# Three TensorE rows of eight instead of four, one uncut last store, and a 1 KB extra store, in a rotary-embedding kernel that streams through memory

## The chip, the core and the metric

The kernel runs on one core of a Trainium2 chip. The metric is device time in microseconds (us). Every quoted time is a median over several executions, each of state "fast", that is, undisturbed. One execution of every kernel was also recorded with the hardware profiler; its "span" runs from the first to the last instruction, and is 1.7 to 2.3 us shorter than the time of the same execution. Engines are named as in the profile: PE is TensorE, PEld its weight loads, DVE is VectorE, ACT is ScalarE, POOL is GpSimd, and SPq is the sequencer of SyncE, which issues the transfers ("DMA").

## The reference

The input `x` is 16 x 512 x 1024 float32, seen as 16 heads of 64. Each head is rotated by a table of cosines and sines of its position:

```python
x1, x2 = x[..., :32], x[..., 32:]          # per head, after the reshape to 16 heads of 64
rotated = np.concatenate([x1 * cos - x2 * sin, x1 * sin + x2 * cos], axis=-1)
```

32 MiB come in and 32 MiB go out, and there is little arithmetic for each byte.

## The kernel before

The work is cut into 8 tiles of 128 partitions x 8192 floats (4 MB). A tile has 8 "rows" of 1024 floats per partition. Each row needs two products and an add: `x * cos`, the half-swapped `x * sin` with signs, and their sum. The rows are spread over the engines in two ways:

```python
PE_ROWS = (0, 2, 4, 6)          # rows whose sum TensorE makes
DVE_B = ((0,), (0, 4))          # rows (even tiles, odd tiles) whose sine product VectorE makes; else GpSimd
LAST_OUT = (4, 8)               # the last tile is stored in two pieces, rows 0-3 and rows 4-7
...
for t in range(NT):
    xt = tiles[t]
    for k in range(KK):
        r = xt[:, k * dim : (k + 1) * dim]
        own = k in DVE_B[t % 2]
        if not own:
            ... nc.gpsimd.tensor_tensor(out=halves(b), ...)                # sine product on GpSimd
        if k in PE_ROWS:
            ps = pe.tile([P, dim], FP32, name="ps")                        # two buffers in PSUM
            nc.vector.tensor_tensor(out=pairs(ps), in0=pairs(r), in1=cos_b(k), op=ALU.mult)
            if own:
                nc.vector.tensor_tensor(out=halves(r), ...)                # sine product on VectorE
            ... nc.tensor.matmul(out=ps[...], lhsT=ident, rhs=rhs, start=False, ...)   # adds it into ps
            nc.scalar.copy(out=r, in_=ps)                                  # ScalarE brings the row back
            while pending: add()
        else:
            while pending: add()
            ps = pd.tile([P, dim], FP32, name="pd")                        # one buffer in PSUM
            nc.vector.tensor_tensor(out=pairs(ps), in0=pairs(r), in1=cos_b(k), op=ALU.mult)
            pending.append((r, ps, b))                                     # add() later: r = ps + b on VectorE
    while pending: add()
    ... store(t)                                                           # the last tile by LAST_OUT
```

All loads and stores are issued by SyncE on one queue. Five tile buffers exist, so tiles 5 to 7 are loaded when the stores of tiles 0 to 2 have landed.

## Time and profile before

| | before |
|---|---|
| time, median of 5 | 163.11 us (163.08 to 163.17) |
| span of the profiled run | 161.6 us |
| data moved on the load/store queue | 67.24 MB |
| VectorE ends its last operation | 142.97 us |
| last store issued (its second half) | 143.03 us |
| last data lands | 160.5 us |

These lines are from the page of the kernel before: busy time by engine, three rows of the 40 slices of the span (a digit is the busy share in tenths; PEclk is the granted TensorE clock in tenths), and the queue that carries loads and stores (packets, MB, share of the 16 DMA engines' span).

```profile
PE 81.8 (51%) x136; PEld 30.3 (19%) x136; DVE 128.9 (80%) x115; ACT 33.7 (21%) x33; POOL 121.0 (75%) x58
...
DVE  1059897999999989999999999999999999930000
...
PEclk9999996559975998799969965999689879995555
DMA  5999999999999999999999999999999999999992
...
q1 hardware_dynamic: 2752, 67.24, 97.5%
```

VectorE, the busiest compute engine, is busy for 80% of the span. The DMA row shows 9 from the second slice to the last but one, while VectorE stops four slices (16 us) earlier. The kernel is bound by the transfers. In the packet records a 32 KB packet takes 1.213 us, and a 4 MB transfer puts 8 of them on each of the 16 engines: 9.7 us per transfer, and sixteen such transfers make 155 us.

The second reading is how much room compute has. The timeline of the kernel before, from 139 us (columns: start, duration, engine and line, operation, operands, count, and in brackets the idle time before it and what ended it):

```profile
139.39 1.96 PE L168 MATMUL ps<-b,ident 128*128 128x512 f32 x4 [1.57 <-DVE ps L163]
...
141.43 1.01 ACT L171 COPY xt<-ps 128x1024 f32<-128x1024 f32 x1 [2.56 <-PE ps L168]
141.74 1.22 DVE L150 TENSOR_TENSOR xt<-pd,b 128x1024 f32<-128x1024 f32 x1
143.03 0.33 SPq L79 DMA_DIRECT2D out_dram<-xt  x1
```

Compute ends at 142.97 us. The store of tile 6 lands at 149.1 to 150.8 us, so the queue gets to the last tile only around 149, and to its second half, the transfer issued at 143.03, about 5 us later. The last tile waits in the queue; the queue doesn't wait for it.

### The profile page before, as it was taken

Reading aid. Unit: us, or ns where it says so; the run is one execution under the profiler, and the core shown is the slowest. Engines: PE = TensorE matmul, PEld = TensorE weight load, DVE = VectorE, ACT = ScalarE, POOL = GpSimd, SP = SyncE. Lnnn points to the kernel's source line nnn. Section 1 sums busy time; section 2 is a strip of 40 time slices with the busy share of each in tenths; the row PEclk is TensorE's granted clock in tenths of the full one; section 3 lists DMA queues with packets and bytes.
Section 4 is the critical chain, followed back from the end, with each engine's and each line's share of the span. In section 5 each row is a group of like instructions: output and inputs, shape, how many; then the busy total and the mean of one; then the engine's idle time right before and its main releaser. Section 6 shows DMA issues by size and latency. Waiting matters only on the chain.

```text
span 161.6 us, 692 instructions
## 1 busy us (share of the span) xinstructions
PE 81.8 (51%) x136; PEld 30.3 (19%) x136; DVE 128.9 (80%) x115; ACT 33.7 (21%) x33; POOL 121.0 (75%) x58
## 2 busy tenths in 40 slices
PE   4136946496429742955097419660984194600000
PEld 1112301241114211311032114210321131100000
DVE  1059897999999989999999999999999999930000
ACT  0003242023302430223113302222223122220000
POOL 1049999999999999999994199999999997000000
PEclk9999996559975998799969965999689879995555
DMA  5999999999999999999999999999999999999992
GB/s 189 395 441 435 454 454 389 446 462 389 438 470 389 389 446 464 389 454 446 397 454 446 397 448 446 406 454 438 406 450 438 406 448 438 414 454 389 438 426 118
DMA packets 2756, 67.28 MB, mean 416 GB/s; under 512 B 320, under 2 KB 448, under 8 KB 448
## 3 DMA queue, kind: packets, MB, share of 16 engines
q1 hardware_dynamic: 2752, 67.24, 97.5%
q8 instruction: 1, 0.02, 0.0%
q14 instruction: 3, 0.02, 0.0%
HBM read 33.69 MB, written 33.55 MB: 416 GB/s over the span
## 4 chain that ended last, share of the span: by engine, by line
DVE 37%; PE 18%; issue 17%; POOL 6%; ACT 4%; DMA 4%; SPq 0%; DVEq 0%; ACTq 0%; POOLq 0%
PE ps L168 17%; DVE xt L150 12%; DVE pd L178 12%; DVE ps L163 7%; POOL b L160 6%; DVE xt L165 5%; ACT xt L171 4%; DMA b<-in_sin_dram 4%; PE tab L110 1%; PE tab L111 1%; DVE tab L118 0%; DVE sns L113 0%; SPq L75 0%; DVE sns L114 0%; DVEq L150 0%
## 5 line engine op out<-in xcount | busy, mean ns | idle before, releaser
L160 POOL TENSOR_TENSOR b<-xt,sns 128x1024 f32<-128x1024 f32 x52 | 120.3, 2350 | 14.5 <-DVE sns L114 9.2
L168 PE MATMUL ps<-xt,ident 128*128 128x512 f32 x48 | 35.8, 888 | 39.2 <-issue 24.5
L171 ACT COPY xt<-ps 128x1024 f32<-128x1024 f32 x32 | 32.4, 1012 | 95.2 <-PE ps L168 90.8
L168 PE MATMUL ps<-b,ident 128*128 128x512 f32 x80 | 43.5, 674 | 14.7 <-DVE ps L163 12.1
L150 DVE TENSOR_TENSOR xt<-pd,b 128x1024 f32<-128x1024 f32 x32 | 39.0, 1218 | 2.2 <-POOL b L160 1.1
L163 DVE TENSOR_TENSOR ps<-xt,tab 128x1024 f32<-128x1024 f32 x32 | 39.1, 1223 | 1.5 <-ACT xt L171 1.3
L178 DVE TENSOR_TENSOR pd<-xt,tab 128x1024 f32<-128x1024 f32 x32 | 39.3, 1227 | 0.8
L168 PEld LDWEIGHTS ps<-b,ident 128*128 128x128 f32 x80 | 17.1, 227 | 44.1 <-issue 30.6
L168 PEld LDWEIGHTS ps<-xt,ident 128*128 128x128 f32 x48 | 11.6, 267 | 58.8 <-issue 46.1
L165 DVE TENSOR_TENSOR xt<-xt,tab 128x1024 f32<-128x1024 f32 x12 | 14.6, 1220 | 0.4
L113 DVE TENSOR_SCALAR sns<-tab 128x256 f32<-128x256 f32 x1 | 0.4, 425 | 8.0 <-PE tab L111 8.0
L171 ACT ACT_TABLE_LOAD x1 | 1.3, 1283 | 13.5 <-DVE xt L165 13.5
L110 PE MATMUL tab<-b,spread 64*128 64x256 f32 x2 | 1.2, 697 | 4.5 <-DMA b<-in_sin_dram 4.5
L101 PE MATMUL ps<-zero 128*128 128x512 bf16 x4 | 1.9, 625 | 1.2 <-DVE zero L97 1.2
L110 PEld LDWEIGHTS tab<-b,spread 64*128 64x128 f32 x2 | 0.5, 308 | 5.4 <-issue 5.4
L111 PE MATMUL tab<-b,spread 64*128 64x256 f32 x2 | 1.1, 631 | 0.0
L97 DVE MEMSET zero<- 128x256 uint32 x1 | 0.3, 272 | 0.9 <-PEq L208 0.9
L101 PEld LDWEIGHTS <-zero 128*128 128x128 bf16 x4 | 0.4, 129 | 1.7 <-DVE zero L97 1.2
L111 PEld LDWEIGHTS tab<-b,spread 64*128 64x128 f32 x2 | 0.7, 333 | 0.2
L118 DVE COPY tab<-sns 128x64 f32<-128x64 f32 x2 | 0.5, 228 | 0.1
L109 DVE COPY spread<-ident 64x64 f32<-64x64 f32 x2 | 0.3, 182 | 0.2 <-POOL ident masks.py:199 0.2
masks.py:197 POOL MEMSET ident<- 128x128 f32 x1 | 0.2, 204 | 0.3 <-POOLq L208 0.3
(6 smaller groups left out, 1.1 us busy)
## 6 DMA issues: line engine op xcount, KB each, us to landing
xt<-in_x_dram SPq DMA_DIRECT2D x7, 4096.0 KB, 29.5
out_dram<-xt SPq DMA_DIRECT2D x7, 4096.0 KB, 30.3
out_dram<-xt SPq DMA_DIRECT2D x2, 2048.0 KB, 18.1
xt<-in_x_dram SPq DMA_DIRECT2D x1, 2560.0 KB, 11.3
xt<-in_x_dram SPq DMA_DIRECT2D x1, 1536.0 KB, 6.2
b<-in_sin_dram SPq DMA_DIRECT2D x1, 64.0 KB, 6.3
b<-in_cos_dram SPq DMA_DIRECT2D x1, 64.0 KB, 6.1
```

The source lines that it names most:

```text
L101: nc.tensor.matmul(out=ps[:, c : c + BANK], lhsT=zero[:, :P], rhs=zero, start=True, stop=True)
L110: nc.tensor.matmul(out=sin_t, lhsT=spread, rhs=sin_sb, start=True, stop=True)
L111: nc.tensor.matmul(out=cos_t, lhsT=spread, rhs=cos_sb, start=True, stop=True)
L113: nc.vector.tensor_scalar_mul(out=sns[:, :, 0, :], in0=sin_k, scalar1=-1.0)
L118: nc.vector.tensor_copy(out=sns_t[:, i * hd : (i + 1) * hd], in_=sns[:, k])
L150: nc.vector.tensor_tensor(out=r, in0=ps, in1=b, op=ALU.add)
L160: nc.gpsimd.tensor_tensor(out=halves(b), in0=swapped(r, nh), in1=over_heads(sk), op=ALU.mult)
L163: nc.vector.tensor_tensor(out=pairs(ps), in0=pairs(r), in1=cos_b(k), op=ALU.mult)
L165: nc.vector.tensor_tensor(out=halves(r), in0=halves(r), in1=swapped_signed(k), op=ALU.mult)
L168: nc.tensor.matmul(out=ps[:, c : c + BANK], lhsT=ident, rhs=rhs, start=False, stop=True, skip_group_check=True)
L171: nc.scalar.copy(out=r, in_=ps)
L178: nc.vector.tensor_tensor(out=pairs(ps), in0=pairs(r), in1=cos_b(k), op=ALU.mult)
```

## The change

Its intent: fewer rows go through TensorE and ScalarE, so that the adds of one more row per tile run on VectorE; the store of the last tile isn't cut; and a 1 KB store of zeros goes out on ScalarE's own queue at the start. The tables' loads are written more plainly, with the same two transfers.

```diff
-PE_ROWS = (0, 2, 4, 6)
+PE_ROWS = (0, 3, 6)
-DVE_B = ((0,), (0, 4))
+DVE_B = ((0,), (0, 3))
-LAST_OUT = (4, 8)
+LAST_OUT = (8,)
-SIN_PARTS = (64,)
-COS_PARTS = (64,)
...
+    zero = fixed.tile([P, BANK], BF16)
+    nc.vector.memset(zero, 0.0)
+    scratch = nc.dram_tensor("scratch", (16, 32), BF16, kind="Internal").ap()
+    nc.scalar.dma_start(out=scratch, in_=zero[:16, :32])
     load(0, 0, FIRST[0])
...
-    zero = fixed.tile([P, BANK], BF16)
-    nc.vector.memset(zero, 0.0)
```

VectorE gets 8 more adds (123 instructions for 115). TensorE has 96 matmul records for rows instead of 128, ScalarE 24 copies instead of 32. GpSimd keeps its 52 products.

More of the change, by code (lines that the diff above doesn't have):

```diff
@@ L83 @@
     cos_sb = bp.tile([P, dim], FP32, name="b")[:PB, : KK * half]
-    for sb, v, parts in ((sin_sb, sin_v, SIN_PARTS), (cos_sb, cos_v, COS_PARTS)):
-        lo = 0
-        for hi in parts:
-            nc.sync.dma_start(out=sb[lo:hi, :], in_=v[lo:hi, :])
-            lo = hi
+    nc.sync.dma_start(out=sin_sb, in_=sin_v)
+    nc.sync.dma_start(out=cos_sb, in_=cos_v)
     for lo, hi in zip(FIRST, FIRST[1:]):
```

## The prediction

> **What bounds the kernel now.** The DMA queue. The page's queue lines give 67.24 MB on one queue, filling 97.5% of the 16 engines' span; the DMA row of the slices is 9 nearly throughout. In the packet records 32 KB takes 1.213 us, so a 4 MB transfer (8 packets per engine) takes 9.7 us, and sixteen make 155 of the 161.6 us. VectorE (80%) and GpSimd (75%) only have to stay ahead. At the end the timeline of SyncE shows the last tile's halves issued at 136.9 and 143.0 us, VectorE ending at 142.97. The queue only gets to the last tile near 148 us (the store before it lands at 149.1 to 150.8), and to its second half near 153. Compute has about 10 us of slack.
>
> **What the change does.**
> - PE rows 2, 4, 6 become 3, 6: one row per tile moves its final add from TensorE and ScalarE to VectorE, 8 more adds. GpSimd keeps 52 products. In the timeline VectorE's operations follow each other at 1.13 us, 1.25 us when one needs the previous one's buffer, 1.33 us when an add directly follows its own product. The new order then makes 17.1 us for an even tile and 18.3 for an odd one, against 15.4 and 16.8 in the last two of before. Tile 0 loses nothing, because GpSimd paces it (products 2.31 us apart). Tiles start at 28.0, 46.4, 63.4, 81.8, 98.8, 117.2, 134.2; VectorE ends near 152.7, 9.7 us later.
> - The earlier stores and reloads still reach the queue in time (store 6 issued near 135, needed near 138).
> - The last tile's row 6 on TensorE starts near 149.1 us after some 4 us idle. Before, bursts after 4.1 us of idle nearly all ran at 0.85 us per matmul, not 0.43. This agrees with the Trainium skill, "TensorE: Matmul & The Clock Gate", Part 1 (half rate after about 3.4 us idle). Then matmuls take 3.7 us and the copy 1.0, ending near 153.9; if warm, VectorE is last at 152.7.
> - One 4 MB last store: nothing leaves until then. Alone it would cost nothing (143 is before 148); with the later compute the queue is empty for 5 to 6 us.
> - The 1 KB store: 16 rows of 64 B on ScalarE's queue, idle until 13.5 us. By the skill's "DMA: Bandwidth & Descriptors", "Issuing engines are not separate DMA queues", it interleaves on the same 16 engines; a 1 KB packet of the tables took 0.046 us here. Under 0.2 us.
>
> **Time.** Store issued 152.7 to 154.0, rather the later; 1.0 us to the first packet (first load: issue 0.73, packet 1.74), 0.5 start-up (first packets took 1.0 us, not 0.46), 9.7 data, 0.4 to the semaphore, 1.1 to the span's end, 1.5 from span to measured time (163.1 against 161.6). That is issue plus 14.2: 166.9 to 168.2. I predict 167.8 us, +2.9%, 8 in 10 between 166.3 and 168.8. Faster by over 2%: 0.01; within 2%: 0.14; slower by over 2%: 0.85.
>
> **What would show it.** VectorE's last add ends near 152.7, ScalarE's last copy after it, the last store is issued near 154; the DMA row dips for 5 to 6 us near 149 to 155, then is full to the end, and 9 elsewhere; 96 row matmuls instead of 128; ScalarE's queue under 0.1%.
>
> **What would make it wrong.** Smaller gaps on VectorE, or GpSimd running differently beside it (1 us of compute is 1 us of time); a warm last burst; the small store disturbing the start.

## The result, and the profile after

| | before | after |
|---|---|---|
| time, median of 5 | 163.11 us (163.08 to 163.17) | 168.19 us (168.02 to 168.40) |
| span of the profiled run | 161.6 us | 166.3 us |
| VectorE ends | 142.97 us | 152.97 us |
| last store issued | 143.03 us | 154.12 us |
| last data lands | 160.5 us | 165.2 us |

The ratio is 1.031, with a 95% interval of 1.030 to 1.033. Ratios here are the mean time of one kernel's fast runs over the mean of the other's fast runs in the same rounds, so they are not quite the ratios of the medians quoted beside them.

The same lines of the page, for the changed kernel (q10 is ScalarE's queue with the 1 KB store):

```profile
PE 83.4 (50%) x104; PEld 26.1 (16%) x104; DVE 139.6 (84%) x123; ACT 25.6 (15%) x25; POOL 121.4 (73%) x58
...
DVE  1069999999999999999999999999999999997000
...
PEclk9999999556785678655559855858555955556755
DMA  6999989898999999999999999999999999960885
...
q1 hardware_dynamic: 2608, 67.24, 94.6%
...
q10 hardware_dynamic: 32, 0.00, 0.0%
```

Three things are to be seen. TensorE was granted its full clock less often (mean 0.69, before 0.83). VectorE works on for two slices and a half longer. And the DMA row has a 6 and a 0 where it had 9s: the queue ran empty near the end, then carried the last store alone. The windows view puts numbers to it. First the kernel before, then the changed one (columns: window, its length, busy us and count of PE, PEld, DVE, ACT, POOL, granted clock, DMA share, GB/s):

```profile
149.00:156.00 7.00, 0.00 (x0) 0.00 (x0) 0.00 (x0) 0.00 (x0) 0.00 (x0) 0.50 0.99 426
156.00:162.00 6.00, 0.00 (x0) 0.00 (x0) 0.00 (x0) 0.00 (x0) 0.00 (x0) 0.50 0.45 191
```

```profile
149.00:156.00 7.00, 3.61 (x4) 1.17 (x4) 3.83 (x4) 1.01 (x1) 0.00 (x0) 0.73 0.17 75
156.00:167.00 11.00, 0.00 (x0) 0.00 (x0) 0.00 (x0) 0.00 (x0) 0.00 (x0) 0.51 0.78 334
```

Between 149 and 156 us the DMA engines were 99% busy before and are 17% busy now, with compute still running in that window. In the packet records the last packets of tile 6's store end at 149.0 us on average over the 16 engines (start 147.8 plus 1.213), the latest at 149.5, and the first packets of tile 7's store begin at 155.0: a hole of 6.0 us on average. The span grew by 4.7 us only, because the slowest engine ends it. Before, the engines had drifted apart, and the last packet ended at 160.1 us, 1.2 us after the mean of the 16 engines' ends (158.9). After the hole all engines start together, and the last packet ends at 164.9, 0.1 us after the mean (164.8). So 1.1 of the 6.0 us are made up by this evening out, 0.2 by tile 6's store having ended earlier (149.0 on average, before 149.2), and the other 4.7 are the growth. The windows view of the changed kernel, which counts a packet where it starts, shows none from 148.4 to 154.9 us:

```profile
148.40:154.90 6.50, 3.61 (x4) 1.17 (x4) 4.43 (x4) 1.01 (x1) 0.00 (x0) 0.67 0.00 0
```

What ended last in the last tile is read from the timeline of the changed kernel:

```profile
149.40 3.61 PE L164 MATMUL ps<-b,ident 128*128 128x512 f32 x4 [2.37 <-DVE ps L159]
...
151.74 1.22 DVE L146 TENSOR_TENSOR xt<-pd,b 128x1024 f32<-128x1024 f32 x1
153.09 1.01 ACT L167 COPY xt<-ps 128x1024 f32<-128x1024 f32 x1 [5.01 <-PE ps L164]
154.12 0.33 SPq L76 DMA_DIRECT2D out_dram<-xt  x1
```

VectorE ends at 152.97 us, but the store waits for ScalarE's copy of row 6, which ends at 154.10, because the four matmuls before it took 3.61 us. The same four took 1.96 us before. This is the half-rate state of the clock, which the Trainium skill describes in "TensorE: Matmul & The Clock Gate", Part 1. The granted clock in the trace is 0.50 until 152.74 us.

### The profile page after: what moved, and what is told of

The parts are those of the page before. It is cut to its first block, busy times and chain, and to the rows that moved or that the text cites. A ratio compares the mean times of both kernels' runs of the same rounds, so it can differ in the third digit from the quotient of the medians.

```text
span 166.3 us, 610 instructions
## 1 busy us (share of the span) xinstructions
PE 83.4 (50%) x104; PEld 26.1 (16%) x104; DVE 139.6 (84%) x123; ACT 25.6 (15%) x25; POOL 121.4 (73%) x58
## 4 chain that ended last, share of the span: by engine, by line
DVE 71%; issue 13%; DMA 4%; PE 3%; ACT 1%; DVEq 0%; SPq 0%; ACTq 0%
DVE pd L174 29%; DVE xt L146 23%; DVE ps L159 10%; DVE xt L161 9%; DMA b<-in_sin_dram 4%; PE ps L164 2%; PE tab L106 1%; ACT xt L167 1%; PE tab L107 1%; DVEq L146 0%; DVE tab L114 0%; DVE sns L109 0%; SPq L72 0%; DVE sns L110 0%; DVEq L161 0%
## 5 line engine op out<-in xcount | busy, mean ns | idle before, releaser
L164 PE MATMUL ps<-xt,ident 128*128 128x512 f32 x48 | 41.6, 1018 | 36.2 <-issue 21.1
L164 PE MATMUL ps<-b,ident 128*128 128x512 f32 x48 | 37.9, 934 | 27.5 <-DVE ps L159 17.2
L146 DVE TENSOR_TENSOR xt<-pd,b 128x1024 f32<-128x1024 f32 x40 | 48.9, 1221 | 2.5
L174 DVE TENSOR_TENSOR pd<-xt,tab 128x1024 f32<-128x1024 f32 x40 | 49.1, 1228 | 1.1
L167 ACT COPY xt<-ps 128x1024 f32<-128x1024 f32 x24 | 24.3, 1012 | 114.8 <-PE ps L164 100.3
L159 DVE TENSOR_TENSOR ps<-xt,tab 128x1024 f32<-128x1024 f32 x24 | 29.3, 1222 | 0.0
L164 PEld LDWEIGHTS ps<-xt,ident 128*128 128x128 f32 x48 | 12.9, 296 | 63.6 <-issue 58.8
L164 PEld LDWEIGHTS ps<-b,ident 128*128 128x128 f32 x48 | 11.7, 268 | 54.4 <-POOL b L156 28.0
```

Source lines behind the costliest of these rows:

```text
L146: nc.vector.tensor_tensor(out=r, in0=ps, in1=b, op=ALU.add)
L164: nc.tensor.matmul(out=ps[:, c : c + BANK], lhsT=ident, rhs=rhs, start=False, stop=True, skip_group_check=True)
```

## The experiments

Theory: the loss is what two parts of the change make together. VectorE's additional adds make the last tile ready some 10 us later, and the uncut store lets nothing of it leave before all of it is ready; only then does the queue run empty. Rivals: (A) the later compute costs its time anyway; (B) the small store, or the lower granted clock with fewer rows on TensorE, costs it; (C) a 4 MB last store costs time by itself. All runs gave the right result, and the kernel before ran beside each (medians 163.25 to 163.32 us).

### One part at a time

**e1_split_last**: the changed kernel, with the store cut again.

```diff
-LAST_OUT = (8,)
+LAST_OUT = (4, 8)
```

> The changed kernel with the last store cut in two again (rows 0-3, rows 4-7). Theory (the loss is the product of later compute and an uncut last store): the first half is issued near 148.1 us, the second near 154.1 as in the changed kernel, but only 4.9 us of data remain behind it; span near 161.8, time 163.4 to 164.0, so -2.6% against the changed kernel. Rival A (the later compute alone costs the time): 167 to 168.2. Rival B (the small store or the lower granted clock costs it): 167.5 to 168.2.

Measured: 163.42 us, ratio to before 1.001 (0.999 to 1.003). VectorE still ends at 152.99 us, and the halves are issued at 147.81 and 153.27. The two windows for this kernel:

```profile
149.00:156.00 7.00, 2.73 (x4) 0.71 (x4) 3.85 (x4) 1.01 (x1) 0.00 (x0) 0.60 0.95 405
156.00:162.00 6.00, 0.00 (x0) 0.00 (x0) 0.00 (x0) 0.00 (x0) 0.00 (x0) 0.50 0.48 205
```

With as late a compute, the DMA share in 149 to 156 us is back at 0.95, because rows 0 to 3 keep the queue busy while rows 4 to 7 are made. Rivals A and B fall: the later compute, the lower clock and the small store are all still there.

**e2_before_one_store**: the kernel before, with the store in one piece.

```diff
-LAST_OUT = (4, 8)
+LAST_OUT = (8,)
```

> The kernel before with nothing changed but the last store in one piece. Theory: it is issued at 143.0 us, the queue gets to it only near 148, so nothing is lost: 163.0 to 163.3. Rival C (one 4 MB store at the end costs time by itself, by its longer tail): 165 to 168.

Measured: 163.17 us, ratio 0.999 (0.998 to 1.001). The store was issued at 143.72 us, and tile 6's store landed at 148.9 to 150.5. Rival C falls. So neither part costs anything alone, and together they cost 5 us.

**e3_before_small_store** and **e4_after_no_small_store**: the 1 KB store put into the kernel before, and taken out of the changed kernel.

```diff
     # e3, into the kernel before (its zeros are made here instead of later):
+    scratch = nc.dram_tensor("scratch", (16, 32), BF16, kind="Internal").ap()
+    nc.scalar.dma_start(out=scratch, in_=zero[:16, :32])
     # e4, out of the changed kernel:
-    scratch = nc.dram_tensor("scratch", (16, 32), BF16, kind="Internal").ap()
-    nc.scalar.dma_start(out=scratch, in_=zero[:16, :32])
```

> The kernel before with nothing changed but the 1 KB store (and its zeros made earlier). Theory: the tables land up to 0.2 us later, the queue stays full: span within 0.2 us of 161.6, time 163.1 to 163.3. Rival D (the second queue costs something outside the span: in the changed kernel time less span was about 2.0 us against 1.8): 163.4 to 163.8 with the span unchanged. Rival B (the small store is the cause): 166 or more.

> The changed kernel without the 1 KB store. Theory: the start is 0.2 us earlier, so the last store is issued near 153.9: time 167.8 to 168.1. Rival D: 167.4 to 167.8. Rival B: 163 to 165.

Measured: e3 163.22 us, ratio 0.999 (0.998 to 1.001); e4 168.35 us, ratio 1.030 (1.028 to 1.032), against 1.031 with the store. e4 is 0.25 us over the range that I named: its last store was issued at 154.24 us, not near 153.9, so leaving the small store out gained nothing at the end. The small store costs nothing that can be seen, inside the span or outside it (rival D of these expectations falls too).

### Which engine is last

**e5_last_row5**: the changed kernel, with row 5 in place of row 6 on TensorE in the last tile alone.

```diff
-            if k in PE_ROWS:
+            if k in ((0, 3, 5) if t == NT - 1 else PE_ROWS):
```

> The changed kernel with rows 0, 3, 5 instead of 0, 3, 6 on TensorE in the last tile alone: as many operations on every engine. Theory (the last store waits for ScalarE's copy after a half-rate burst, 154.1 us, while VectorE is done at 152.97): now VectorE's last add, near 153.0, is last: the last store is issued 1.0 to 1.2 us earlier, time 167.0 to 167.3. Rival (VectorE's end alone sets it and the copy is a bystander): 168.0 to 168.4.

Measured: 167.23 us, ratio 1.024 (1.023 to 1.026). From the timeline of this kernel:

```profile
149.51 1.01 ACT L167 COPY xt<-ps 128x1024 f32<-128x1024 f32 x1 [1.50 <-PE ps L164]
...
151.67 1.23 DVE L146 TENSOR_TENSOR xt<-pd,b 128x1024 f32<-128x1024 f32 x1
152.96 0.33 SPq L76 DMA_DIRECT2D out_dram<-xt  x1
```

Now ScalarE's copy is done at 150.52 us and VectorE is last. The store leaves 1.16 us earlier and the time falls by 0.96 us. So about 1 us of the 5 is the slow last burst on TensorE with the copy behind it, and the rest is VectorE's.

### How much delay is free

**e6_first4** and **e7_first6**: three rows in the first 4 or 6 tiles only, four rows (with the division of work of before) in the rest; the store uncut.

```diff
-PE_ROWS = (0, 3, 6)
+def pe_rows(t):
+    return (0, 3, 6) if t < THREE_UNTIL else (0, 2, 4, 6)      # THREE_UNTIL = 4 in e6, 6 in e7
...
-DVE_B = ((0,), (0, 3))
+def dve_b(t):
+    return (0,) if t % 2 == 0 else (0, 3) if t < THREE_UNTIL else (0, 4)
...
```

> The changed kernel with three rows on TensorE in tiles 0 to 3 and the four of before in tiles 4 to 7; last store in one piece. Theory of the slack: compute ends near 147.3 us, and the queue is busy with the store before until 148.6 to 149.5, so half of the delay costs nothing: 163.0 to 163.5. Rival (each extra add costs its share, linear in the number of tiles): half of 5.1 us, 165.6.

> The same with three rows in tiles 0 to 5 and four in tiles 6 and 7. Theory: compute ends near 150.0 us, 0.8 us to the first packet, about 1.5 us of empty queue: span near 162.2, time 163.7 to 164.3. Rival (linear): 6/8 of 5.1 us, 166.9.

Measured: e6 163.28 us, ratio 1.000 (0.999 to 1.001); e7 164.51 us, ratio 1.007 (1.006 to 1.009), 0.2 us over the range named. Half of the tiles cost nothing, two more cost 1.2 us, and the last two 3.7. The cost isn't a sum over tiles; it begins at a threshold.

**e9_idle_vector_op**: the kernel before with its four rows, the store uncut, and one idle product per tile on VectorE. It tests whether VectorE's time alone does it, with TensorE's work as it was.

```diff
+    junk = fixed.tile([P, dim], FP32)
+    nc.vector.memset(junk, 0.0)
...
+            if k == 3:
+                nc.vector.tensor_tensor(out=pairs(junk), in0=pairs(junk), in1=cos_b(k), op=ALU.mult)
```

> The kernel before, four rows on TensorE, last store in one piece, no 1 KB store; one idle VectorE product per tile on a tile of zeros that nobody reads. Theory (VectorE's own time moves the last store, whatever TensorE does): compute ends 7 to 8 us later than with one store alone (143.7), near 150.7 to 151.7; last store issued then; 12.2 us to the span's end and 1.8 more: time 164.7 to 165.8. Rival (taking rows off TensorE, with the lower granted clock, is what costs time): 163.1 to 163.4, as with one store alone.

Measured: 163.06 us, ratio 0.998 (0.997 to 1.000). My expectation was wrong: VectorE ended at 148.58 us, not 150.7 to 151.7. The starts of its operations in the trace show why. I had put the idle product between an add and a product that had to wait for that add's buffer. Before, the product followed the add after 1.25 us; now all steps there are 1.13, so an idle product adds 1.01 us where it stands, and in several tiles it also filled a wait for ScalarE. The store was issued at 148.64 us, in time. The run can't tell the theory from the rival.

**e11_idle_vector_more**: the same with four more idle products, so that compute does end late.

```diff
-            if k == 3:
+            if k == 3 or (k == 6 and t >= 4):
```

> The same as the run with one idle VectorE product per tile, with a second one in tiles 4 to 7 ahead of row 6's product: 4 times 1.13 us more, so VectorE ends near 153.1 us (148.6 there), as late as in the changed kernel, with all four rows still on TensorE. Theory (the moment at which the last tile is ready decides): last store issued 153.2, or up to 154.2 if the last burst runs at half rate; time 167.2 to 168.2. Rival (fewer rows on TensorE, or the lower granted clock, is the cause): 163.1 to 163.4.

Measured: 167.56 us, ratio 1.026 (1.024 to 1.028), single runs from 167.03 to 168.38. The timeline and the windows of this kernel:

```profile
149.29 3.75 PE L172 MATMUL ps<-b,ident 128*128 128x512 f32 x4 [0.91 <-DVE ps L167]
...
151.64 1.22 DVE L152 TENSOR_TENSOR xt<-pd,b 128x1024 f32<-128x1024 f32 x1
153.13 1.01 ACT L175 COPY xt<-ps 128x1024 f32<-128x1024 f32 x1 [3.69 <-PE ps L172]
154.16 0.33 SPq L79 DMA_DIRECT2D out_dram<-xt  x1
```

```profile
149.00:156.00 7.00, 3.75 (x4) 1.17 (x4) 3.73 (x4) 1.45 (x2) 0.00 (x0) 0.50 0.19 80
156.00:167.00 11.00, 0.00 (x0) 0.00 (x0) 0.00 (x0) 0.00 (x0) 0.00 (x0) 0.50 0.78 334
```

All four rows are on TensorE and the mean granted clock is 0.82, near the 0.83 of before (the changed kernel had 0.69), yet the hole and the loss are there. It is the moment at which the last tile is ready that decides, and not which engine made it late. The single runs have spans of 165.3 to 165.6 or of 166.0 to 166.6 us; a last burst at full or half rate would explain that, but only one run has a trace, so it isn't shown.

All runs with an uncut last store can now be put in one table, by the moment at which it is issued:

| kernel | last store issued, us | issue plus 12.2 us | span, us | ratio to before |
|---|---|---|---|---|
| e2 | 143.72 | 155.9 | 161.1 | 0.999 |
| e6 | 147.58 | 159.8 | 161.4 | 1.000 |
| e9 | 148.64 | 160.8 | 161.3 | 0.998 |
| e7 | 150.53 | 162.7 | 162.7 | 1.007 |
| e5 | 152.96 | 165.2 | 165.1 | 1.024 |
| after | 154.12 | 166.3 | 166.3 | 1.031 |
| e11 | 154.16 | 166.4 | 166.3 | 1.026 |
| e4 | 154.24 | 166.4 | 166.4 | 1.030 |

The 12.2 us are read from the changed kernel: 0.84 to the first packet, 9.9 for the packets, 0.37 to the last semaphore, 1.08 to the end. Up to an issue near 149 us the span is that of the busy queue; after that it is the issue plus 12.2. The threshold follows from the packets of the runs that lost nothing (e2, e6, e9, before): there the slowest engine is done with tile 6 at 150.0 to 150.4 us, and 0.84 us before that is 149.2 to 149.6. The mean engine is done at 149.1 to 149.2 already. That the slowest one counts is seen in e9, whose engines stood empty for 0.5 us on average before the last store, the slowest not at all, and nothing was lost.

### A version that tries to beat both

**e8_split_3_6_8**: the changed kernel's compute, no small store, the last tile in three pieces that are each ready before the queue is empty.

```diff
-LAST_OUT = (8,)
+LAST_OUT = (3, 6, 8)
```

> The changed kernel without the 1 KB store, last store in three pieces: rows 0-2 (ready near 144), 3-5 (near 150.5), 6-7 (near 153.9). Theory: each piece is issued before the queue has emptied, so there is no gap at all, and the queue ends earlier than before because fewer instruction fetches hold up single engines: span 160.2 to 161.0, time 161.9 to 162.8, level with or slightly under the kernel before. Rival (later compute costs time however the store is cut): 165 or more.

Measured: 162.99 us, ratio 0.998 (0.997 to 0.9995), span 161.2. The pieces were issued at 144.49, 150.62 and 154.05 us. From its page:

```profile
DMA  5999999999999999999999999999999999999993
```

The hole is gone, as with e1. The gain that I hoped for from fewer instruction fetches came in the span only: the profiled run is 0.2 us above the range that I named, but the median span of the five runs is 160.8 us, inside it, against 161.5 for the kernel before in the same rounds. Whether the fetches did that was not tested. Time less span was 2.05 to 2.19 us instead of 1.73 to 1.83 and took half of it back, so the time is 0.2 us above its range. The kernel is level with before (under 2% counts as level here), and at best 0.3% faster.

**e10_first6_split**: e7 with the store in three pieces and no small store.

```diff
-LAST_OUT = (8,)
+LAST_OUT = (3, 6, 8)
-    scratch = nc.dram_tensor("scratch", (16, 32), BF16, kind="Internal").ap()
-    nc.scalar.dma_start(out=scratch, in_=zero[:16, :32])
```

> Three rows on TensorE in tiles 0 to 5, four in 6 and 7, last store in three pieces, no 1 KB store. Compute ends near 150.4 us; pieces ready near 141, 147, 150.4, all before the queue gets to them: span near 161.0. Time less span was 1.98 to 2.3 us in the kernels with three rows in all tiles and 1.74 to 1.9 in the others; if that goes with the late instruction fetch (after the span's end in the former), this kernel has 1.8: time 162.7 to 162.9. If it goes with three rows or with the cut store, it has 2.1: 163.0 to 163.2. Either way level with the kernel before (163.3).

Measured: 163.31 us, ratio 1.000 (0.998 to 1.002), span 161.4. The time is outside both of the narrow ranges named. Time less span was 1.86 to 1.92 us, nearer to the first. No version was found that clearly beats the kernel before; with the queue full from 2 to 160 us, moving compute about can't give much.

## Why the prediction was right

- **What bounds it: right.** The queue was full before and is full again wherever the last tile comes in time (e1, e2, e6, e8).
- **VectorE's delay: right.** Predicted: 17.1 us per even tile, 18.3 per odd one, end near 152.7. Measured: 17.08 (tile 2), 18.35 (tile 1), end at 152.97. The tiles start 0.2 to 0.33 us after the predicted times. The sum of observed start-to-start times, by what each operation depends on, held for an order of operations that had not yet run.
- **Stores before the last in time: right.** Store 6 was issued at 134.72 us (predicted near 135), and the hole comes only after it.
- **The last store: right, and shown by parts.** Uncut alone costs nothing (e2), late compute alone costs nothing (e1), both make a hole: 6.0 us on average over the DMA engines, where 5 to 6 were predicted. That the span grows by less than the hole (4.7 us) was not foreseen.
- **The slow last burst: the effect right, its reason wrong.** I wrote that the burst would start "after some 4 us idle". TensorE had been idle for 2.37 us, because the burst before it had itself run at half rate. It ran at half rate all the same, 3.61 us for four (3.7 predicted), and the copy ended at 154.10 (153.9 predicted). By the windows view the granted clock was 0.50 throughout 135 to 149 us, so it had already been at half rate, and no new idle stretch was needed. That it was slow in this run is in part luck: in e1, with the same compute, the same four matmuls took 2.73 us. e5 shows that this burst costs about 1 us.
- **The sum from issue to time: right by two errors that cancel.** I had 14.2 us; the profiled run has 168.40 less 154.12, which is 14.28. But the "0.5 start-up" wasn't there (the packets of the last store took 9.9 us from first start to last end), the first packet came after 0.84 us and not 1.0, and time less span was 2.1 us and not 1.5. The 1.5 was a slip: I took the span of one run from the median time of others; in the profiled run of before it is 163.37 less 161.58, 1.8 us.
- **The small store: right.** Under 0.2 us predicted, nothing seen (e3, e4). I had not foreseen that it takes a completion semaphore from the set that the loads share: the load of tile 4 is issued at 7.23 us instead of 4.53, after the first load has landed. It was needed only at about 42 us.

## What to carry to other kernels

When one queue is full all the time, an engine that gets slower is free until it delivers later than the queue would have taken the data; so compute the moment at which the queue's slowest engine gets to the last transfer, and compare it with the moment at which that transfer's data is ready. The size of the last transfer decides when it can start: a cut that costs nothing while compute is early is what pays for compute that is late, and the two should be judged together, not one by one. Where several engines finish the last tile, ask which of them is last, and put the one with the uncertain duration early.

## What the Trainium skill lacked or had wrong

- "DMA: Bandwidth & Descriptors", section "Bandwidth", says in one place that for transfers between HBM and SBUF the HBM side binds at about 358 GB/s, and in another that a core whose neighbour is idle was measured at 425 GB/s. Here one core alone moved 426 to 437 GB/s in full windows, loads and stores alike (32 KB in 1.213 us on each of 16 engines), so the 358 did not bind this core. The same section's 435 GB/s for the port side is what this agrees with.
- The same page, section "Issuing engines are not separate DMA queues", says that transfers of all issuers interleave on the same engines. That agrees, but it gives no time for a small store behind full queues: 1 KB in 16 rows, issued at 1.16 us on ScalarE's queue, put its first packet on an engine at 5.19 us and landed 5.6 us after its issue, while each of its packets took 0.011 us.
- "TensorE: Matmul & The Clock Gate", Part 1, has the half rate return after an idle window of about 3.4 us, and the full rate after a busy one, with windows that run freely. This case agrees: changes of the clock in a trace lie multiples of 3.41 us apart, and of the bursts of the last tile (3.75, 3.75 and 3.61 us, with pauses of 2.4 us between them) the first two lay across a border of windows and filled at most 2.6 us of any one, while the third filled nearly all of one and was followed by the full clock at 152.74. What the page lacks is how full a window has to be. In the 13 traces (some 490 windows), a window at half rate was followed by the full clock where matmuls filled 0.82 of it or more, and by half rate at 0.78 or less; one at full clock kept it at 0.42 or more and lost it at 0.40 or less. The ends of matmuls are modelled, so these shares are rough.
- "Runtime: NRT & Kernel Launch", "Instruction fetch mechanics", calls the cost of crossing an instruction block mostly hidden. For the engines that may be so, but in a kernel whose transfers are full such a fetch holds up one DMA engine: beside fetches at 64.3 and 96.9 us in the kernel before, single packets took 1.56 us instead of 1.21. Time less span was 1.98 to 2.32 us in most runs of the kernels with 609 to 613 instructions (one run: 1.90), where a 16 KB fetch falls after the span's end, and 1.73 to 1.92 us in those with 630 to 703; that goes together in these runs, but its cause wasn't tested.
- "VectorE: DVE Perf Modes" gives durations of operations, but neither it nor another page gives start-to-start times by dependence: for 128x1024 float32 they were 1.13 us without one, 1.25 us where the buffer of the operation before is needed again, and 1.33 us where an add reads the product just made.
